# A 3-D average pooling kernel: a tiny load ahead of the first one, and one real store in place of three tiny ones on ScalarE's queue

## The chip, the cores and the metric

The kernel runs on one core of one Trainium2 chip. The metric is the device time of one execution in microseconds (us); lower is better. Before the change it is 91.98 us, the median of 5 runs (91.95, 91.96, 91.98, 92.26, 92.50).

## The reference

The input x has the shape (8, 32, 32, 32, 32) in float32, 33.55 MB. Each output element is the mean of a 2 x 2 x 2 block of the last three dimensions, so the output has the shape (8, 32, 16, 16, 16), 4.19 MB.

```
for i in range(out_d):
    for j in range(out_h):
        for k in range(out_w):
            window = x[:, :, 2*i:2*i+2, 2*j:2*j+2, 2*k:2*k+2]
            result[:, :, i, j, k] = np.mean(window, axis=(-3, -2, -1))
```

## The kernel before

Batch and channel together are 256 rows of 32,768 elements. They are worked on as two halves of 128 rows, t = 0 and t = 1, one row per SBUF partition. The loop over `plan` (lines 71 to 82) goes through each half in four pieces of 8 depth planes, 32 KB per row and 4 MB in all. Six of the pieces are loaded by one DMA; the last two, of t = 1, by two DMAs of 2 MB each, which makes ten loads. All are issued by SyncE (SP) at line 77, in the order of the plan, into five buffers named `tin`; a load into a buffer that was used before waits until VectorE is done with it.

For each loaded part `pool_unit` (lines 53 to 69) does three VectorE steps: it adds neighbouring depth planes (line 58), adds neighbouring columns (line 62), and adds neighbouring rows with a scale of 1/8 into the output buffer `obuf0` or `obuf1` (line 65). The profile shows the last step as two instructions, the second of which writes `dummy`. Each output buffer holds 128 rows of 4,096 elements, counted in 16 units of 256 elements (KF). A 4 MB piece fills four of these units.

The stores come after the loop. At line 88 ScalarE's queue issues three tiny ones: 16 rows of 128 elements (512 B) each, from unit 0 of `obuf0`, unit 8 of `obuf0` and unit 0 of `obuf1`. They write the right values, but to places that the stores of line 92 write again. Those are issued by SP: all of `obuf0` (2 MB), the first 14 units of `obuf1` (1.75 MB), and its last 2 units (0.25 MB). The framework orders the instructions and sets the semaphore waits. Each DMA announces its landing on one of eight semaphores, which are handed out in turn, so a later DMA also waits for the landing of the one that had its semaphore before it. Since the tiny stores and SP's stores write the same places, SP's also wait for the tiny ones.

Behind that, `tile_avg_pool_3d_kernel` edits the program. Lines 107 to 114 take the first load out of the main block and put it into the opening block, ahead of SP's part of the barrier at which all engines start together; so load 1 is the first thing that SP does, and load 2 comes after the barrier. The rest of the function takes the waits for the stores out of the closing barrier, and puts them at the very end of SP's program, one for each semaphore that a store uses.

Of the kernel before, what the change touches and what calls it, by code (L numbers as in the profile page):

```python
# [1 line left out]

# [4 lines left out]

F32 = mybir.dt.float32
KF = 256


@with_exitstack
def pool_rows(
    ctx: ExitStack,
    tc: tile.TileContext,
    x: bass.AP,
    kernel_size: int,
    out: bass.AP,
):
    nc = tc.nc  # L20
    assert kernel_size == 2, "only kernel_size == 2 supported"

    B, C, D, H, W = x.shape
    P = nc.NUM_PARTITIONS
    assert (B * C, D, H, W) == (2 * P, 32, 32, 32)
    add = mybir.AluOpType.add

    xv = x.rearrange("b c d h w -> (b c) (d h w)")  # L30
    ov = out.rearrange("b c d h w -> (b c) (d h w)")

    pool_in = ctx.enter_context(tc.tile_pool(name="pin", bufs=5))
    pool_out = ctx.enter_context(tc.tile_pool(name="pout", bufs=1))
    obuf = [pool_out.tile([P, 16 * KF], F32, name=f"obuf{t}") for t in range(2)]
    dummy = pool_out.tile([P, 1], F32, name="dummy")


    plan = [
        (0, 0, (32,)),
        (0, 32, (32,)),
        (0, 64, (32,)),
        (0, 96, (32,)),
        (1, 0, (32,)),
        (1, 32, (32,)),
        (1, 64, (16, 16)),
        (1, 96, (16, 16)),  # L50
    ]

    def pool_unit(buf, t, k0, kb):

        od = kb // 8
        a = buf.rearrange("p (o dd e) -> p o dd e", o=od, dd=2)
        b = buf[:, :od * 1024]
        nc.vector.tensor_add(  # L58
            out=b.rearrange("p (o e) -> p o e", o=od), in0=a[:, :, 0], in1=a[:, :, 1])
        bv = b.rearrange("p (e ww) -> p e ww", ww=2)  # L60
        c = buf[:, od * 1024:od * 1536]
        nc.vector.tensor_add(out=c, in0=bv[:, :, 0], in1=bv[:, :, 1])  # L62
        cv = c.rearrange("p (j hh k) -> p j hh k", hh=2, k=16)
        o0 = k0 * KF // 8
        nc.vector.tensor_tensor_reduce(  # L65
            out=obuf[t][:, o0:o0 + od * 256].rearrange("p (j k) -> p j k", k=16),
            in0=cv[:, :, 0], in1=cv[:, :, 1],
            scale=0.125, scalar=0.0, op0=add, op1=add, accum_out=dummy[:, :],
        )

    for t, k0, parts in plan:
        tin = pool_in.tile([P, 32 * KF], F32, tag="tin", name="tin")
        views = []
        o = 0
        for kb in parts:
            v = tin[:, o * KF:(o + kb) * KF]
            nc.sync.dma_start(
                out=v, in_=xv[t * P:(t + 1) * P, (k0 + o) * KF:(k0 + o + kb) * KF])
            views.append((v, k0 + o, kb))
            o += kb  # L80
        for v, k, kb in views:
            pool_unit(v, t, k, kb)

    for t, k0 in [(0, 0), (0, 8), (1, 0)]:
        nc.scalar.dma_start(
            out=ov[t * P:t * P + 16, k0 * KF:k0 * KF + 128],
            in_=obuf[t][:16, k0 * KF:k0 * KF + 128])  # L90
    for t, k0, kb in [(0, 0, 16), (1, 0, 14), (1, 14, 2)]:
        nc.sync.dma_start(
            out=ov[t * P:(t + 1) * P, k0 * KF:(k0 + kb) * KF],
            in_=obuf[t][:, k0 * KF:(k0 + kb) * KF],
        )


def kernel(tc: tile.TileContext, x: bass.AP, kernel_size: int, out: bass.AP):
    nc = tc.nc
    pool_rows(tc, x, kernel_size, out)  # L100
    tc.close()
    tc.compile()  # L102
    blocks = nc.main_func.blocks

    opening, program = blocks[0].instructions, blocks[tc.starting_block_idx].instructions
    load = next(i for i in program if isinstance(i, mybir.InstDMACopy))
    assert load.engine == nc.sync.engine
    barrier = next(  # L110
        n for n, i in enumerate(opening)
        if i.engine == load.engine and isinstance(i, mybir.InstDrain))
    program.remove(load)
    opening.insert(barrier, load)

    closing = blocks[-1].instructions
    stores = [  # L120
        i for i in program
        if isinstance(i, mybir.InstDMACopy) and "out_" in i.outs[0].memref]
    kept = [u.id for i in stores for u in i.sync_info.on_update]
    kept = [n for j, n in enumerate(kept) if n not in kept[j + 1:]]
    final = next(
        i for i in closing
        if i.engine == nc.sync.engine and isinstance(i, mybir.InstDrain))
    waits = {w.id: w for w in final.sync_info.on_wait}
    closing[closing.index(final)] = mybir.InstDrain(
        name=final.name, engine=final.engine, ins=[], outs=[], is_reset_sema=False,  # L130
        sync_info=mybir.SyncInfo(
            on_wait=[w for n, w in waits.items() if n not in kept], on_update=[]))


    reset = next(
        n for n, i in enumerate(closing)
        if isinstance(i, mybir.InstDrain) and i.is_reset_sema)
    first, stop = closing[reset].reset_range_start, closing[reset].reset_range_stop
    assert isinstance(closing[reset + 1], mybir.InstISA)
    while len(closing) > reset:  # L140
        closing.pop()
    n = first
    while n < stop:
        m = n
        while m < stop and m not in kept:
            m += 1
        if m > n:
            closing.append(mybir.InstDrain(
                name=nc.get_next_instruction_name(), engine=nc.gpsimd.engine, ins=[], outs=[],
                is_reset_sema=True, reset_range_start=n, reset_range_stop=m))  # L150
            nc.gpsimd.sem_clear(range(n, m))
        n = m + 1
    for n in kept:
        w = waits[n]
        closing.append(mybir.InstEventSemaphore(
            name=nc.get_next_instruction_name(), engine=nc.sync.engine, ins=[], outs=[],
            sync_info=mybir.SyncInfo(
                on_wait=[w],
                on_update=[mybir.SyncUpdate(
                    sync_type="semaphore", id=n, ant_name=w.ant_name,  # L160
                    update_mode="sem-sub-imm", update_value=w.wait_value)])))


# [1 line left out]
_INS = ['x', 'kernel_size']  # L165
_OUTS = [((8, 32, 16, 16, 16), 'float32')]

_NUMBERS = {'kernel_size': 2}


# [26 lines left out]
```

## Time and profile before

| | |
|---|---|
| median of 5 runs | 91.98 us |
| the profiled execution's own time | 91.98 us |
| its span, first to last recorded instruction | 86.3 us |
| VectorE busy | 64.0 us (74%) |
| read from and written to HBM, as recorded | 33.55 MB, 4.22 MB |
| load 1: issued, landed | 0.00, 12.04 us |
| loads 2 to 6 landed | 21.74, 31.47, 41.19, 50.91, 60.63 us |
| loads 7 to 10 (2 MB each) landed | 65.53, 70.42, 75.32, 80.84 us |
| tiny stores issued | 20.1, 39.5, 59.0 us |
| SP's stores issued | 49.26, 81.04, 85.24 us |
| SP's stores landed | 85.69, 90.03, 90.58 us |

All times count from the first recorded instruction, which is the issue of load 1. A landing is the last of the sixteen semaphore updates of a DMA, one from each DMA engine. The span is shorter than the execution's time, since it ends with the last recorded instruction: the last store is still under way then, and its wait at the very end of SP's program is not recorded.

How to read the page: a line of digits divides the span into 40 slices, each digit being the busy share in tenths (9 is 90% or more). A group of instructions shows its line, engine and tiles, then the busy time, the mean of one in ns, and the engine's idle time before the group with what ended it. A DMA line shows the size and the time from issue to landing. In the chain of work that ended last, a row is a start, a length and what it was. In the table of stretches, a row is a window, its length, the busy time of each engine, the granted TensorE clock (TensorE is not used here), the mean busy share of the 16 DMA engines and what they moved. In short stretches that share can be over 1, since a packet counts where it begins. q1 is SP's DMA queue and q10 ScalarE's.

### The profile page before, as it was taken

How to read it: one execution, taken by the hardware profiler on the slowest of the kernel's cores; microseconds unless marked ns; L12 is line 12 of the kernel's file. 1: busy time of each engine (PE TensorE's matmuls, PEld its weight loads, DVE VectorE, ACT ScalarE, POOL GpSimd, SP SyncE). 2: the span in 40 equal slices, each digit the busy share in tenths (PEclk: the TensorE clock that was granted, in tenths of full speed). 3: DMA queues.
4: the chain of work that ended last, by engine and by line, in shares of the span. 5: the costliest groups of instructions: out<-in, count | busy, mean ns of one | idle time of the engine just before them, and what ended most of it. 6: DMA issues, size and time to landing. Idle time of an engine off the chain costs nothing.

```text
span 86.3 us, 94 instructions
## 1 busy us (share of the span) xinstructions
DVE 64.0 (74%) x40; POOL 0.2 (0%) x4
## 2 busy tenths in 40 slices
DVE  0000049993999739993899839993899999999994
POOL 0000000000000000000000000000000000000000
DMA  8889997999979997999979997998999999999999
GB/s 243 365 365 486 486 486 319 410 486 486 427 306 486 486 486 334 395 486 486 441 323 456 486 486 334 395 486 365 465 390 471 395 463 387 471 395 327 463 403 426
DMA packets 1727, 36.35 MB, mean 421 GB/s; under 512 B 224, under 2 KB 272, under 8 KB 272
## 3 DMA queue, kind: packets, MB, share of 16 engines
q1 hardware_dynamic: 1631, 36.33, 99.1%
q10 hardware_dynamic: 96, 0.02, 0.1%
HBM read 33.55 MB, written 4.22 MB: 438 GB/s over the span
## 4 chain that ended last, share of the span: by engine, by line
DMA 61%; DVE 37%; issue 0%; DVEq 0%
DMA tin<-in_x_dram 61%; DVE tin L58 21%; DVE tin L62 11%; DVE obuf L65 6%; DVE dummy L65 0%; DVEq L102 0%
## 5 line engine op out<-in xcount | busy, mean ns | idle before, releaser
L58 DVE TENSOR_TENSOR tin<-tin 128x4096 f32<-128x4096 f32 (+1 forms) x10 | 35.7, 3569 | 20.6 <-DMA tin<-in_x_dram 20.6
L62 DVE TENSOR_TENSOR tin<-tin 128x2048 f32<-128x2048 f32 (+1 forms) x10 | 18.6, 1864 | 0.3
L65 DVE CUSTOM_DVE_ANT_1 obuf<-tin 128x1024 f32<-128x1024 f32 (+1 forms) x10 | 10.1, 1011 | 0.3
L65 DVE DVE_READ_ACCUMULATOR2_ANT dummy<- 128x1 f32 x10 | 0.8, 82 | 0.0
L178 POOL MEMSET const-bfloat16-1.0<- 128x1 bf16 x1 | 0.1, 102 | 0.0
L178 POOL MEMSET const-uint8-127<- 128x1 uint8 x1 | 0.1, 102 | 0.0
L178 POOL MEMSET const-float32-1.0<- 128x1 f32 x1 | 0.1, 99 | 0.0
L178 POOL MEMSET const-float32-0.0<- 128x1 f32 x1 | 0.1, 98 | 0.2 <-issue 0.2
## 6 DMA issues: line engine op xcount, KB each, us to landing
tin<-in_x_dram SPq DMA_DIRECT2D x6, 4096.0 KB, 34.9
tin<-in_x_dram SPq DMA_DIRECT2D x4, 2048.0 KB, 37.7
out_dram<-obuf SPq DMA_DIRECT2D x1, 2048.0 KB, 36.4
out_dram<-obuf SPq DMA_DIRECT2D x1, 1792.0 KB, 9.0
out_dram<-obuf SPq DMA_DIRECT2D x1, 256.0 KB, 5.3
out_dram<-obuf ACTq DMA_DIRECT2D x3, 8.0 KB, 6.4
```

The costliest lines, as they stand in the source:

```text
L58: nc.vector.tensor_add(out=b.rearrange("p (o e) -> p o e", o=od), in0=a[:, :, 0], in1=a[:, :, 1])
L62: nc.vector.tensor_add(out=c, in0=bv[:, :, 0], in1=bv[:, :, 1])
L65: nc.vector.tensor_tensor_reduce(out=obuf[t][:, o0:o0 + od * 256].rearrange("p (j k) -> p j k", k=16), in0=cv[:, :, 0], in1=cv[:, :, 1], s ...
L178: nc = _bacc.Bacc("TRN2", target_bir_lowering=False, num_devices=1)
```

## The change

A new tile `first` of 16 rows by 128 elements is loaded on SP's queue, from the first 16 rows of x, ahead of the loop. Nothing reads it. The edit of the opening block now moves two loads ahead of the barrier: this one, and behind it the first 4 MB load. At the end the three tiny stores on ScalarE's queue are gone. ScalarE's queue issues one real store instead, of units 0 and 1 of `obuf1` with all 128 rows (0.25 MB), which are ready when the fifth piece is done. SP's stores are all of `obuf0` as before, units 2 to 13 of `obuf1` (1.5 MB), and units 14 and 15 as before. So no place is written twice.

```diff
     dummy = pool_out.tile([P, 1], F32, name="dummy")
+    first = pool_out.tile([16, 128], F32, name="first")
+    nc.sync.dma_start(out=first[:, :], in_=xv[:16, :128])
...
-    for t, k0 in [(0, 0), (0, 8), (1, 0)]:
-        nc.scalar.dma_start(
-            out=ov[t * P:t * P + 16, k0 * KF:k0 * KF + 128],
-            in_=obuf[t][:16, k0 * KF:k0 * KF + 128])
-    for t, k0, kb in [(0, 0, 16), (1, 0, 14), (1, 14, 2)]:
-        nc.sync.dma_start(
+    for queue, t, k0, kb in [
+        (nc.scalar, 1, 0, 2),
+        (nc.sync, 0, 0, 16),
+        (nc.sync, 1, 2, 12),
+        (nc.sync, 1, 14, 2),
+    ]:
+        queue.dma_start(
             out=ov[t * P:(t + 1) * P, k0 * KF:(k0 + kb) * KF],
             in_=obuf[t][:, k0 * KF:(k0 + kb) * KF],
         )
...
-    load = next(i for i in program if isinstance(i, mybir.InstDMACopy))
-    assert load.engine == nc.sync.engine
-    barrier = next(
-        n for n, i in enumerate(opening)
-        if i.engine == load.engine and isinstance(i, mybir.InstDrain))
-    program.remove(load)
-    opening.insert(barrier, load)
+    loads = [i for i in program if isinstance(i, mybir.InstDMACopy)][:2]
+    assert [i.outs[0].bass_ap.tensor.name.split("_")[0] for i in loads] == ["first", "tin"]
+    for load in loads:
+        assert not load.sync_info.on_wait
+        barrier = next(
+            n for n, i in enumerate(opening)
+            if i.engine == load.engine and isinstance(i, mybir.InstDrain))
+        program.remove(load)
+        opening.insert(barrier, load)
```

## The prediction, made before the changed kernel ran

> **What bounds the kernel now.** I read the page first, then the chain of work that ended last, the table of busy time by stretch, the DMA view of the first 5 us, and the issue and landing times of each transfer.
>
> ```profile
> DVE 64.0 (74%) x40; POOL 0.2 (0%) x4
> DMA  8889997999979997999979997998999999999999
> q1 hardware_dynamic: 1631, 36.33, 99.1%
> q10 hardware_dynamic: 96, 0.02, 0.1%
> L58 DVE TENSOR_TENSOR tin<-tin 128x4096 f32<-128x4096 f32 (+1 forms) x10 | 35.7, 3569 | 20.6 <-DMA tin<-in_x_dram 20.6
> out_dram<-obuf SPq DMA_DIRECT2D x1, 1792.0 KB, 9.0
> out_dram<-obuf SPq DMA_DIRECT2D x1, 256.0 KB, 5.3
> ```
>
> VectorE is busy 74% and its idle time is all waiting for loads; SP's queue, q1, keeps the 16 DMA engines at work for 99.1% of the span; the three tiny stores, q10, take 0.1%. So the DMA engines are the resource that is full. The chain ends in VectorE work, which could mislead:
>
> ```profile
> 20.11 40.52 DMA tin<-in_x_dram
> ...
> 60.65 4.44 DVE tin L58
> ```
>
> From 60.65 to 85.21 the chain is VectorE alone. But the span stops before the last bytes land. The 2 MB store was issued at 49.26 and landed 36.4 later, at 85.69; the 1.75 MB store was issued at 81.04 (when VectorE finished its columns) and landed at 90.03; the 0.25 MB store was issued at 85.24 and landed at 90.58. Each landed one transfer time after the one ahead (4.34 and 0.55 us), so each stood in a queue that never ran dry: the 1.75 MB store had over 4 us in hand at its issue, the last one over 4 us too. VectorE may be later by some 3.5 us at the end and nothing moves. The end is start of the stream + bytes at the DMA rate + 1.40 us (91.98 of the profiled execution less 90.58). That execution's 91.98 is also the median of the five runs.
>
> ```profile
> core 0: us, DVE busy (x) POOL busy (x), PEclk, DMA share, GB/s
> 0.00:1.00 1.00, 0.00 (x0) 0.20 (x4) 1.00 0.00 0
> ...
> 12.00:40.00 28.00, 23.85 (x12) 0.00 (x0) 1.00 1.00 431
> ...
> 76.00:80.00 4.00, 3.93 (x5) 0.00 (x0) 1.00 0.97 365
> 80.00:86.30 6.30, 5.11 (x7) 0.00 (x0) 1.00 1.00 427
> ```
>
> The share is 1.00 nearly everywhere. Two stretches are weak: the first microsecond, and 76 to 80, where load 10 gives way to the first store (365 GB/s). The start, closer, in 40 slices of 0.125 us:
>
> ```profile
> DMA  0000000099987006000000999900000099990000
> ```
>
> It counts a packet where it begins: nothing for eight slices. The packet records say more. Load 1 is issued at 0.00; its first packets (32 KB, one per DMA engine) begin between 1.03 and 1.95 and take 1.21 to 2.02 us, where all later ones take 1.213. The mean excess is 0.56 us. They end together, 2.76 to 3.19, whenever they began.
>
> **The change, part by part.**
>
> *The tiny load ahead of load 1.* SP issues it at 0.00. Before, the first issue took 0.385, and the gap to the next in back-to-back issues is 0.05 (0.791 + 0.332 to 1.173). The tiny stores, also 16 rows, took 0.32 to 0.38 to issue, so few rows make an issue no shorter. Load 1 is issued at 0.385 + 0.05 = 0.44 in place of 0.00; the largest step between two back-to-back issues, 0.535 (1.647 to 2.182), is the upper bound. Nothing stands ahead of load 1 to hide this: the DMA engines are idle, so the whole stream moves with it. What may give it back is the cold start. If the 0.56 us excess is paid once, by whichever transfer is first, the tiny load pays it from 1.03 on and load 1 starts warm: 0.44 - 0.56 = -0.12. If also the 1.03 us from issue to first packet is partly paid once, load 1's packets begin no later than before, and the gain is up to 0.56; the far bound is packets that begin right at the end of load 1's own issue, 0.44 + 0.385 = 0.82, and end at 2.03 instead of the median 3.07: -1.0. No row shows a second transfer on an idle queue, so the bounds are -1.0 and +0.54. I take +0.44, since the excess goes with all 16 engines starting at once (the one that began at 1.95 had none), which load 1 does again; a 16-row transfer cannot do that for it.
>
> The Trainium skill speaks against the change here: DMA: Bandwidth & Descriptors, section Latency and other measured facts, gives every transfer on this path a first-byte latency of about 0.6 us and a tiny one at least 0.8 us, as a fixed cost of each and not of the first alone. By that rule load 1 pays its latency again behind the tiny load, and the term is the full issue time. A once-only cost would make it about zero or below. The trace has only one cold start and can't say which.
>
> *SP's other instructions.* SP reaches the start barrier 0.44 us later, and load 2 goes out at about 1.23 instead of 0.79. It is needed when load 1's packets run out, near 11 us. Cost 0. Loads 6 to 10 wait for VectorE or for the landing of an earlier transfer (load 10 was issued at 41.21, just behind landing 4 at 41.19); with another number of transfers those pairs shift. At 41 us loads 5 and 6 alone held work until 60.63, so an issue some 19 us later is still covered. Cost 0. SP's waits before the stores for the tiny stores' landings go, since the new ScalarE store shares no rows and columns with SP's; they bound nothing.
>
> *Three tiny stores out.* Each gives a DMA engine one 512 B packet of 27 ns and a 4 B one of 9 ns: 3 x 36 = 0.11 us less. In the loads' landings they leave no trace: the distances are 9.70, 9.73, 9.72, 9.72, 9.72. Take -0.11.
>
> *256 KB moved from SP's store to ScalarE's queue.* On ScalarE it is ready where the third tiny store was, 58.98; nothing is queued behind it on that engine. Per DMA engine it is 8 packets of 2 KB: 84 ns each by the last store's rows, plus 9, so 0.68 us, inserted among loads 7 and 8. SP's store loses as much: rows of 12,288 B instead of 14,336 B. Rows of 14,336 take 535 ns and of 16,384 take 611, so I estimate 459 for 12,288: 8 x (535 - 459) = 0.61 less. Net +0.07. The loads behind it land 0.7 us later, and VectorE with them; the 3.5 us in hand cover that. If they did not, the excess would come out at the end one to one.
>
> *The tiny load's own packets*: 27 + 9 ns, before load 1 streams. 0.04 at most.
>
> *Reading SBUF amid loads.* Before, the change of direction from loads to stores costs: at 77.55 to 79.5 two or three packets of every DMA engine took 0.67 to 1.05 us instead of 0.61, 0.47 us per engine in sum. The new store reads SBUF amid loads. The nearest row is the third tiny store, whose packets took 27 to 33 ns with no slow neighbours. Bounds: 0 and one such turn, 0.47; if each of its 8 packets paid a turn it would be 3.8. I take 0.05, near the tiny stores.
>
> **Sum:** +0.44 - 0.11 + 0.07 + 0.04 + 0.05 = +0.49, from 91.98 to 92.47.
>
> **The rivals.** A change of over 0.5%, 0.46 us, is about what a measurement of this kernel can tell from none; the borders are 91.52 and 92.44.
>
> *Forecast: the start is simply later.* +0.35 to +0.65, or 92.33 to 92.63. For it: nothing ahead of load 1 hides an issue, and DMA has no slack. Chance 0.55; it straddles the border, so 0.36 slower, 0.19 same.
>
> *Covered start.* The first packets ended together although they began 0.9 us apart, as if held until about 1.8 by something common. If that is released by the tiny load as early as before, load 1's packets, now beginning at 1.47 or later, lose little: 0 to 0.2, or 92.0 to 92.2. Chance 0.13, all same.
>
> *The other side: the first transfer pays a once-only cost.* Load 1's packets begin near 1.03 again and run at 1.213 from the first: -0.56 + 0.05 for the rest, 91.47; to 91.2 if they begin earlier still. It decides from the point where over 0.9 us of the 1.59 (1.03 + 0.56) is once-only: 0.44 to make good the later issue, 0.46 to pass the border. For it: an excess that only the first packets have. Against it: the last engine to begin had none. Chance 0.23, of it 0.20 faster.
>
> *The ScalarE store pays for its turns.* From +0.47 on top of the forecast, 92.9, to 95 or more with eight turns. Against it: the tiny stores paid nothing. Chance 0.09, slower.
>
> Together: faster 0.20, same 0.19 + 0.13 + 0.03 = 0.35, slower 0.36 + 0.09 = 0.45. The range leaves out the store's turns and the lowest of the once-only case: 91.4 to 92.8.
>
> **What would show it.** Load 1's issue at 0.4 to 0.5, its first packets' begin near 1.5 and their end near 3.5 mean the forecast; an end near 3.1 the covered start; an end near 2.5 with packets of 1.213 the once-only cost. Later landings of loads should be 9.72 apart, except some 0.7 more around 62 to 66. Slow packets around 62 to 64 mean that the store pays turns. The last landing should come at about 91.1, with 1.4 behind it. I am wrong if the weak stretch at 76 to 80 goes or another opens, or if a store's issue comes after the one ahead has landed.

## The result, and the profile after

The changed kernel takes 92.32 us (median of 30 runs, 92.06 to 92.86) against 92.03 us (median of 58 runs, 91.75 to 92.50). The ratio is 1.0033, with a 95% interval of 1.0025 to 1.0042: 0.30 us slower, which is real but under the 0.46 us that the prediction set as its border. The forecast was 92.47, its own range 92.33 to 92.63. As a change, +0.49 was forecast from 91.98, and +0.30 came, from 92.03.

The profiled execution took 92.74 us, 0.42 over the median, so sums over its whole length exaggerate. A second profile of the same kernel (e9 below) was taken in an execution of 92.21, close to the median.

These are the page's lines that answer to those shown of before:

```profile
DVE 64.0 (73%) x40; POOL 0.2 (0%) x4
...
DMA  7599989999799969996999799996999999999999
...
q1 hardware_dynamic: 1662, 36.23, 98.1%
q10 hardware_dynamic: 144, 0.26, 0.8%
...
L60 DVE TENSOR_TENSOR tin<-tin 128x4096 f32<-128x4096 f32 (+1 forms) x10 | 35.7, 3570 | 21.9 <-DMA tin<-in_x_dram 21.9
...
out_dram<-obuf SPq DMA_DIRECT2D x1, 1536.0 KB, 8.4
out_dram<-obuf ACTq DMA_DIRECT2D x1, 256.0 KB, 9.6
out_dram<-obuf SPq DMA_DIRECT2D x1, 256.0 KB, 4.8
first<-in_x_dram SPq DMA_DIRECT2D x1, 8.0 KB, 1.5
```

The two DMA queues together are at work for 98.9% of the span, VectorE has not changed, and the ScalarE store takes 9.6 us to land, at 69.86, between loads 7 (67.35) and 8 (72.41). The chain of waits (start, length, what) shows what the change put in front:

```profile
0.00 0.38 SPq L41
0.38 0.05 issue
0.44 12.11 DMA tin<-in_x_dram
```

The tiny load's issue takes 0.38, the next instruction follows after 0.05, and load 1 goes out at 0.44. From its issue to its landing load 1 needs 12.11, so nothing is gained behind the tiny load; before it needed 12.04:

```profile
0.00 12.04 DMA tin<-in_x_dram
```
The first 5 us of the DMA engines in the changed kernel, in 40 slices of 0.125 us, counted where a packet begins:

```profile
DMA  0000000011099998060000000699990000069999
```

The two 1s are the tiny load's packets, from 1.01 on. Load 1's first group of 9s stands in the slices from 1.375 to 1.875; before, the first 9s stood from 1.0 to 1.375. The packet records give 1.48 to 2.24 for the beginnings (before: 1.03 to 1.95) and 3.50 for the median end (before: 3.07), +0.43. The mean excess over 1.213 is 0.56 us, as before.

By stretch (window, length, VectorE and GpSimd busy, clock, DMA share, GB/s), first the page's execution, then the second profile, then the one stretch of before that the prediction doesn't show:

```profile
12.00:40.00 28.00, 23.50 (x11) 0.00 (x0) 1.00 1.00 420
...
76.00:80.00 4.00, 3.93 (x5) 0.00 (x0) 1.00 1.04 446
```

```profile
12.00:40.00 28.00, 23.81 (x12) 0.00 (x0) 1.00 1.02 438
...
60.00:64.00 4.00, 2.61 (x1) 0.00 (x0) 1.00 0.83 336
...
76.00:80.00 4.00, 3.93 (x5) 0.00 (x0) 1.00 1.05 451
```

```profile
60.00:64.00 4.00, 3.35 (x1) 0.00 (x0) 1.00 1.03 436
```

The weak stretch of before at 76 to 80 (365 GB/s) is gone in both. Other weak ones have come: 12 to 40 in the page's execution (420, before 431), and 60 to 64 in the second profile (336, before 436), where the ScalarE store stands. The last store landed at 91.35 and 90.82, after 90.58 before; behind it come 1.39 us in both, 1.40 before.

### The profile page after: what moved, and what is told of

It is laid out like the page before. It is cut to its first block, busy times and chain, and to the rows that moved or that the text cites. A ratio compares the mean times of both kernels' runs of the same rounds, so it can differ in the third digit from the quotient of the medians.

```text
span 87.5 us, 91 instructions
## 1 busy us (share of the span) xinstructions
DVE 64.0 (73%) x40; POOL 0.2 (0%) x4
## 4 chain that ended last, share of the span: by engine, by line
DMA 61%; DVE 37%; SPq 0%; issue 0%; DVEq 0%
DMA tin<-in_x_dram 61%; DVE tin L60 20%; DVE tin L64 11%; DVE obuf L67 6%; SPq L41 0%; DVE dummy L67 0%; DVEq L104 0%
```

## The experiments

The theory: the DMA engines are never idle, so load 1's issue, 0.44 later, comes out at the end one to one, and the stores change almost nothing. The rivals: a cold start that the first transfer pays once; and stores that give or take something. Each run is set against the kernel before, run beside it on the same chip, so the median of before differs a little from one to the next; an interval is one of 95%.

**The tiny load alone** (e1, and again as e8): the kernel before, with these lines of the change and its loop over two loads in the opening block.

```diff
+    first = pool_out.tile([16, 128], F32, name="first")
+    nc.sync.dma_start(out=first[:, :], in_=xv[:16, :128])
```

> The tiny load ahead of load 1 alone, all else as before. If the later issue is passed on one to one, +0.44 us (ratio 1.0048), with load 1's first packets beginning at about 1.48 and still taking 1.5 to 2.0 us. If the measured +0.30 of the whole change is the start's true price, because some of the cold start is given back, +0.30 (1.0033) here and nothing from the stores. If the start is covered, 0.

Measured: 92.77 against 92.01, ratio 1.0082 (1.0065 to 1.0100), from 6 runs. That is +0.75, more than any theory gave, and +0.75 with the stores' -0.15 (e2 below) doesn't add up to the whole change's +0.30. So it was run again, on one chip with the whole change and the stores alone.

> The tiny load alone once more, beside the whole change and the stores alone on one chip. Its first price, +0.75, is 0.3 over the 0.44 of load 1's later issue, and does not add up with the stores' -0.15 to the +0.30 of the whole change. If the 0.3 was a scatter of packets slowed in those executions, +0.44 now (ratio 1.0048). If it belongs to this kernel, +0.75 again (1.008).

Measured: 92.56 against 92.04, ratio 1.0057 (1.0041 to 1.0074), +0.52. Load 1 was issued 0.44 late in both. e8's interval, +0.38 to +0.68 us, includes 0.44; e1's doesn't. The profiles show slow packets, not a still later start: all packets after 4 us, set against the usual time of their size, lost 1.09 and 0.78 us per DMA engine, where before lost 0.56. In both, 0.62 of it stands in the last loads before the first store (before 0.47); the rest is scattered.

**The tiny load, no tiny stores, SP's stores as before** (e10).

> The tiny load ahead, no tiny stores, and SP's stores as before. If the issue is all, +0.44 less up to 0.11: +0.33 to +0.44 (1.0036 to 1.0048). If the tiny load and the tiny stores make each other dearer, +0.3 or less here, against +0.75 with the tiny stores.

Measured: 92.58, ratio 1.0053 (1.0033 to 1.0073), +0.49. The tiny stores are not what makes the tiny load dear. The last loads before the first store lost 0.65 here.

**The tiny load behind load 1** (e4): e1 with one edit.

```diff
-    for load in loads:
+    for load in loads[::-1]:
```

> The same tiny load, but issued just behind load 1, both ahead of the barrier. It delays load 2's issue alone, which has about 10 us in hand. If the price is the delay of load 1's issue, +0.04 (its packets' 36 ns) or 1.000; if it is another DMA, its semaphore or the pairing of semaphores, about as much as with the tiny load ahead, +0.3 to +0.44.

Measured: 92.04 against 92.01, ratio 1.0004 (0.9994 to 1.0015), +0.04. In its page the tiny load now stands in the queue and lands when load 1 does:

```profile
first<-in_x_dram SPq DMA_DIRECT2D x1, 8.0 KB, 11.7
```

The same transfer with the same semaphore costs nothing that can be measured once load 1 goes first. The price is the place in front.

**Four tiny loads ahead** (e5), of rows 0 to 63, 16 each.

```diff
+    for n in range(4):
+        first = pool_out.tile([16, 128], F32, name=f"first{n}")
+        nc.sync.dma_start(out=first[:, :], in_=xv[n * 16:(n + 1) * 16, :128])
```

> Four tiny loads ahead of load 1. Load 1 is issued at about 1.75, after the first tiny load has landed (1.5). If every issue delays the stream one to one and nothing is paid once, 4 x 0.44 = +1.75 us (ratio 1.019), and load 1's first packets, from 2.8 on, still exceed 1.213 by 0.5 to 0.6 on average. If the excess or the 1.03 us to the first packet is paid once, by a first transfer that has come back, +0.7 to +1.2, with first packets of 1.21.

Measured: 93.84 against 91.94, ratio 1.0197 (1.0174 to 1.0221), +1.81. The chain of waits shows the four issues and load 1 behind them, 1.81 late:

```profile
0.00 0.38 SPq L42
0.38 0.06 issue
0.44 0.41 SPq L42
0.85 0.04 issue
0.89 0.42 SPq L42
1.31 0.04 issue
1.35 0.42 SPq L42
1.77 0.04 issue
1.81 12.05 DMA tin<-in_x_dram
```

The first tiny load had landed at 1.66, before load 1 went out. Yet load 1 needs 12.05 to land, as cold as ever. Its first packets begin at 2.88, 1.06 after its issue, with a mean excess of 0.65. The DMA engines' first 5 us show the four small groups and a long gap ahead of load 1:

```profile
DMA  0000000010001001100110099970000000000999
```

So the rival of a once-only cost falls, as far as tiny loads on SP's queue can tell. (The ratio's interval allows +1.60 to +2.03; only four runs were taken.)

**The tiny load on ScalarE's queue** (e6), beside load 1 and not ahead of it.

```diff
+    nc.scalar.dma_start(out=first[:, :], in_=xv[:16, :128])
```

> The tiny load goes out on ScalarE's queue ahead of the barrier, so that SP issues load 1 at about 0.0 and both start together. If the price is SP's issue time alone, 1.000 (+0.04 for its packets). If two issues at once share what makes the descriptors, load 1's packets begin later by up to 0.4: up to +0.4. If a tiny load can warm the start, faster than before, by up to 0.56.

Measured: 92.08 against 91.94, ratio 1.0013 (0.9997 to 1.0028), +0.12: no gain, and at most a small loss. Load 1's first packets begin at 1.01 and end at a median of 2.99. Between the price of 36 ns of packets and a small sharing of the start it does not decide.

**No tiny stores** (e3): the loop of three tiny stores is deleted.

> The three tiny stores left out, and nothing put in their place. By packet time 3 x 36 ns less per DMA engine: -0.11 (ratio 0.9988). If they cost nothing, 1.000; if they warm something for the real stores, slower than before, above 1.001.

Measured: 92.00 against 92.01, ratio 0.9999 (0.9986 to 1.0012): 0, and the predicted -0.11 is still just inside the interval.

**Six tiny stores** (e7).

```diff
-    for t, k0 in [(0, 0), (0, 8), (1, 0)]:
+    for t, k0 in [(0, 0), (0, 4), (0, 8), (0, 12), (1, 0), (1, 4)]:
```

> Six tiny stores in place of three, one at each 4 unit step. If each costs its 36 ns per DMA engine, +0.11 (ratio 1.0012). If they are hidden, 1.000; if each costs more than its packets (a turn from loading to storing), more than +0.15.

Measured: 92.16 against 91.94, ratio 1.0017 (1.0005 to 1.0029), +0.16 for three more. The interval, +0.05 to +0.27, holds the +0.11 of 36 ns each; no gain shows.

**The new stores alone** (e2, and again as e11): the kernel before, with the change's list of stores and without the tiny load.

```diff
+        (nc.scalar, 1, 0, 2),
+        (nc.sync, 0, 0, 16),
+        (nc.sync, 1, 2, 12),
+        (nc.sync, 1, 14, 2),
```

> The new set of stores alone, no tiny load. By my sum -0.11 for the tiny stores, +0.07 for the smaller packets, up to +0.05 for reading SBUF amid loads: 0.0 (ratio 1.000). If the start costs its full 0.44 in the changed kernel, the rest must have given back 0.14: -0.14 (0.9985). If the new store pays turns, over +0.3.

> The new set of stores alone, once more: -0.15 (0.9984) if the first measurement holds, 0 if it was chance.

Measured: 91.87, ratio 0.9984 (0.9970 to 0.9997), -0.15; then 91.77, ratio 0.9967 (0.9954 to 0.9980), -0.30. The gain is there both times. Without the tiny stores alone it was 0 (e3), so the likelier source is the 256 KB on ScalarE's queue. That is argued and not shown: e3's interval reaches -0.13, and no run has the ScalarE store beside the tiny stores. In e11's stretches:

```profile
60.00:64.00 4.00, 3.09 (x1) 0.00 (x0) 1.00 0.99 418
...
76.00:80.00 4.00, 3.93 (x5) 0.00 (x0) 1.00 1.00 389
```

Something is lost while the new store is under way (418, before 436), and less than before is lost at the change to SP's stores (389, before 365). In e2's profile the second is not so: its packets lost 0.51 us there, before 0.47.

**The changed kernel once more** (e9), no edit.

> The changed kernel once more. If the parts add, it is the tiny load's price of this call less 0.15. By its first measurement +0.30 (1.0033). Its profile should show the weak stretch where loads give way to stores, some 0.5 us per DMA engine around 78, which all other profiles have and its first profile lacks; if it lacks it again, the change removes it.

Measured: 92.22 against 92.04, ratio 1.0026 (1.0012 to 1.0040), +0.24. On this chip the parts add: e8's +0.52 for the tiny load and e11's -0.30 for the stores make +0.22. Its weak stretch at 76 to 80 is missing again, as shown above.

**The changed kernel with the tiny load behind load 1** (e12): the edit of e4, on the changed kernel.

> The changed kernel with one edit: the tiny load goes out behind load 1, so the same set of transfers, but load 1 at 0.00. If the delay of load 1 is the whole price of the tiny load, this is the new stores alone: -0.15 to -0.30 (ratio 0.9967 to 0.9984). If the missing stretch of slow packets before the first store comes from this set of transfers, and is worth its 0.47, -0.6 to -0.8 (0.992) and no slow packets around 78; if it comes from the later start, the slow packets are back. If the tiny load has a price of its own, 0 or above.

Measured: 91.78 against 91.98, ratio 0.9979 (0.9965 to 0.9992), -0.19. Against the changed kernel's two ratios, 1.0033 and 1.0026, this one edit is worth 0.54% and 0.47%, 0.43 to 0.50 us: the issue time again. It and the stores alone beat both kernels, the one before by 0.15 to 0.30. Its stretches:

```profile
60.00:64.00 4.00, 3.34 (x1) 0.00 (x0) 1.00 0.99 388
...
76.00:80.00 4.00, 3.93 (x5) 0.00 (x0) 1.00 1.03 438
```

The weak stretch at 76 to 80 is gone here too, with load 1 at 0.00, so the later start is not what removed it. And removing it is not worth its 0.47: the loss now stands at 60 to 64 (388), where the ScalarE store is.

## Why the prediction was right in its way and too high by 0.15

**What bounds the kernel: right.** Wherever load 1 went out later, the end came later, by up to 1.8 us (e5). VectorE's later work did not matter: in the changed kernel SP's 1.5 MB store was issued at 82.37, while the store ahead of it landed at 87.11, so the queue still had over 4 us in hand.

**+0.44 for load 1's later issue: right.** It was issued at 0.436, its first packets ended 0.43 later, four of them cost +1.81, and the place behind load 1 cost +0.04. The tiny load alone, with SP's old stores, cost 0.05 to 0.31 more than that (e1, e8, e10). In all three profiles the last loads before the first store lost 0.15 to 0.18 us more per engine than before, and e1 lost more elsewhere too. Why stays open.

**The excess of the first packets is not paid once: right.** It was 0.56 before, 0.56 after and 0.65 behind four tiny loads. From issue to first packet load 1 took 1.03, 1.05 and 1.06. The reason that I gave, all 16 engines starting at once, was not tested by itself. Load 1's issue took 0.385, 0.41 and 0.42 of these times, so from its end 0.65, 0.64 and 0.64 were left. The Trainium skill, DMA: Bandwidth & Descriptors, section Latency and other measured facts, gives DMAs on this path (sync and scalar) about 0.6 us to the first byte. Counted from the end of the issue the trace agrees, behind tiny loads too; counted from its start the measured time is longer.

**The stores: here the prediction failed.** The terms -0.11 for the tiny stores, +0.07 for smaller packets and +0.05 for reading SBUF amid loads gave +0.01. Measured were -0.15 and -0.30. The packet times were right: rows of 12,288 B took 460 ns against the estimate of 459, those of 2,048 B took 84. Wrong was the step "Reading SBUF amid loads", which allowed only a cost, from 0 up, with no bound on the side of a gain: if the other two terms hold, -0.11 and -0.26 are left for it, in place of +0.05.

Where the gain comes from stays open. The store does pay: the stretch 60 to 64 lost 0.08 and 0.05 us per DMA engine with the new stores alone, and 0.13, 0.18 and 0.33 in the changed kernel's two profiles and e12 (before 0.01). In the same order, the last loads before the first store lost 0.51, 0.35, 0.00, 0.00 and 0.04, in 16 KB packets from 74 us on that took over 0.66 us instead of 0.61 (before 0.47). But over all packets after 4 us the five lost 0.66, 0.48, 1.12, 0.57 and 0.49, against 0.56 before. So most of the loss is moved, and two profiles alone show a saving, of 0.07 to 0.08.

These sums are means over the 16 engines, while the time goes by the engine that ends last: in all fourteen profiles the execution's time is the last landing and 1.38 to 1.40 us more. The last store has one semaphore update per engine. Before, their mean came at 90.23 and the last at 90.58; in the second profile of the changed kernel at 90.70 and 90.82. So the mean engine ended 0.47 later there, close to the +0.49 of the sum, and the last one only 0.24 later, since the engines ended closer together. The first profile shows the same small distance, 91.22 and 91.35. The prediction had no term for this. With one or two executions profiled of each kernel it is not shown to be the source of the gain.

**No cost elsewhere: right.** Load 2's issue at 1.26, the barrier and the shifted pairs of semaphores cost nothing that e4 can measure (+0.04). The waits that went are also in e12, which is faster than the kernel before.

**The rivals.** The covered start and the once-only cost fell with e5 and with the changed kernel's own first packets. The store that pays for its turns is half true: it pays 0.05 to 0.33 us per engine, but the time doesn't rise with it. The sum, +0.44 and -0.15 to -0.30, gives +0.14 to +0.29, against +0.24 and +0.30 measured. With the tiny load's price as measured alone, the sums are +0.60 (e1 and e2) and +0.22 (e8 and e11), so how well the parts add is not settled. That 92.47 came so near is partly luck: the tiny load alone cost up to 0.31 more than forecast, and the stores cost 0.16 to 0.31 less.

**A misreading.** The prediction says that two or three packets of every engine were slow before the first store. The records show 28 slow packets on 16 engines, one or two each; their sum, 0.47 us per engine, is right.

**Signs named in advance.** Load 1 at 0.4 to 0.5 and first packets from about 1.5 to about 3.5: seen. A weak stretch at 76 to 80 that goes, and another that opens: seen too, and named as a way to be wrong. Whether the miss came from there is not shown. Loads 7 and 8 together took 0.72 longer in the second profile, where some 0.7 was named.

## What to carry to other kernels

Where the DMA engines are full from the first packet to the last, ask what is issued ahead of the first load: here each tiny load there cost its whole issue time, some 0.44 us, though it moved only 8 KB, and behind load 1 it cost nothing measurable. A tiny transfer didn't warm the start for the next one, so look in the trace for whether the next transfer starts cold again before you pay for a warm-up. When a change has two parts, time them apart: here one lost 0.5 to 0.75 us and the other gained 0.15 to 0.30, and the better kernel was one of the parts. And where 16 engines share the work, look at the one that ends last besides the mean.

## What the runs showed of the hardware that was not expected

Ahead of the first store, while the last load is still landing, the DMA engines lose 0.35 to 0.65 us each on average, mostly in one to three slow packets. It stands at about 77 to 80 us in eleven of the fourteen profiles (in e5, where everything is 1.8 later, at 79 to 81), and is missing in the changed kernel's two and all but missing in e12's. In these three the tiny load and the 256 KB ScalarE store are both present, and ScalarE's store stands in a weak stretch of its own. With either alone it is there. Why it goes only with both stays open.
